# One encoder layer on one core: the first w_ff2 loads wait for a square, and three unused tiles shift addresses

## The chip, the cores and the metric

The kernel runs on one core of a Trainium2 chip. The metric is device time in microseconds (us) from launch to end. A change counts as seen when it goes beyond 0.5%, about what a measurement of this kernel can tell from no change.

## The reference

Input x is 512 tokens by 1024 channels in float32. After a first layer norm one projection of 11,328 columns feeds two branches: 2-D neighbourhood attention (16 heads) and a bidirectional state-space mixer (SSD, 8 groups of 256 channels, each followed by its share of the product with w_ssd_br). Both are merged by sigmoid gates and go through w_o; then comes

```python
h = layer_norm(DN_ALPHA * h + mix, ln1_g[l], ln1_b[l])
h = layer_norm(DN_ALPHA * h + sq_relu_mlp(h, w_ff1[l], w_ff2[l]), ln2_g[l], ln2_b[l])
# sq_relu_mlp(x, w1, w2) = square(relu(x @ w1)) @ w2, w1 1024x4096, w2 4096x1024
```

## The kernel before, in words

**Precision.** Each float32 operand of the large products is split into a high part (rounded to the type fp32r by a copy on ACT) and a low part (the rest, a subtraction on DVE or POOL). `mm3` (lines 351 to 354) then issues three matmuls: high by high, low by high, high by low. In the profile's rows the moving operand is named first behind the arrow and the stationary one second.

**The SSD stage** is planned by the class `Plan`, which orders operations by given costs and issues them in that order. `gated_norm` writes the two halves of a group's result to yTh and yTl; `ssd_branch` multiplies them, as the moving operand (128x512), with w_ssd_br into the banks ps_sbr: 8 groups x 8 output tiles x 2 x 3 = 384 matmuls.

**The MLP** is everything from line 1389. w_ff1 is taken in four quarters of 1024 hidden channels, each in four slabs of 256 columns. `split_weights` loads a slab with one 1 MB DMA on SP's queue into a tile with the tag ws (two buffers), then splits it in two halves: ACT (L341) the high, DVE (L342) the low. `ff1_tile` multiplies 128 hidden channels by all tokens (24 matmuls into one of two banks tagged mm), ACT takes the relu out of the bank (L1554) and the square (L1560) into r2. A bank is free for the next tile but one when its relu is done.

w_ff2 is multiplied by `ff2_strassen` for the first two quarters together (h = 0) and for the third (h = 1), by Strassen's scheme: seven products, in the order 3, 6, 2, 4, 1, 5, 7, in which the squares, or differences of two blocks of squares, are the stationary operand (tiles sqh and sql) and blocks of w_ff2, or sums of two, the moving one. At h = 0 a product has two steps, c = 0 and 1; a step is 24 matmuls. The fourth quarter is done plainly, with gh and gl.

A block of w_ff2 is loaded by `block` (L1448): 1 MB on POOL's queue into a tile w2r. Where a product needs a sum of two blocks, `plus` (L1454) adds the second with two DMAs of 512 KB that accumulate in place; POOL issues them when the first block has landed, so they hold up what follows on POOL's queue. The tiles w2r come from two buffers of their own (tag wr) and, each third one, from the ws buffers that the w_ff1 slabs use too. The first three blocks are those of product 3, step 0 (wr), product 3, step 1 (ws) and product 6, step 0 (wr).

The order within each engine outside the SSD stage is chosen by the framework, which simulates the program and puts what is ready first; each engine then runs its list strictly in order. So a load may be placed well ahead of where the program text has it, and an instruction that waits holds up all that stand behind it on its engine.

**Addresses.** [...] In the kernel before, yTh and yTl begin 64 bytes past a multiple of 128, the four buffers that hold sqh and sql 96 past one, mgh and mgl (the stationary operands of the product with w_o) 96 past one. hTh, hTl, h1Th, h1Tl, aTh, aTl, hBh, hBl, gh, gl and all tiles wh and wl but one pair (one slab of w_o) begin at multiples of 128. The rows of all these tiles are whole multiples of 128 bytes.

Of the kernel before, what the change touches and what calls it, by code (L numbers as in the profile page):

```python
# [11 lines left out]
F32 = mybir.dt.float32  # L12
# [7 lines left out]
P = 128  # L20
# [292 lines left out]
def encoder_layer(ctx, tc, x, w_in, w_attn_br, w_ssd_br, w_o, w_ff1, w_ff2, pcols, rows64,  # L313
                  d_skip, ln_rows, rpb_pad, consts, lmask, out, dbg=None):
    nc = tc.nc
# [11 lines left out]
    def split_weights(parts, nk, ncol, name, hi, lo, eng=nc.vector, pool=None, after=None):  # L327


        st = (pool or wp).tile([P, nk, ncol], F32, tag="ws", name=f"ws_{name}")  # L330
        c = 0
        for src, r0, c0, n in parts:
            nc.sync.dma_start(
                st[:, :, c : c + n],
                src[r0 : r0 + nk * P, c0 : c0 + n].rearrange("(k p) c -> p k c", p=P),
            )
            c += n
        hk = nk // 2
        for i, k in enumerate((slice(0, hk), slice(hk, nk))):
            with tc.issue_after(after[i]) if after else ExitStack():  # L340
                nc.scalar.activation(hi[:, k], st[:, k], AF.Copy)  # L341
            (eng[i] if isinstance(eng, tuple) else eng).tensor_tensor(out=lo[:, k], in0=st[:, k], in1=hi[:, k].bitcast(F32),  # L342
                              op=ALU.subtract)
        return hi, lo
# [6 lines left out]
    def mm3(o, lh, ll, rh, rl, start, stop):  # L351
        nc.tensor.matmul(o, lh, rh, start=start, stop=False)  # L352
        nc.tensor.matmul(o, ll, rh, start=False, stop=False)  # L353
        nc.tensor.matmul(o, lh, rl, start=False, stop=stop)  # L354
# [45 lines left out]
    gcp = gc.__enter__()  # L400
# [3 lines left out]
    gep = ge.__enter__()  # L404
# [2 lines left out]
    ident = cst[:, CC_ID : CC_ID + P]  # L407
    tri_f = cst[:, CC_TF : CC_TF + P]
    tri_b = cst[:, CC_TB : CC_TB + P]
    ones = gcp.tile([P, P], F32, name="ones")  # L410
    nc.vector.memset(ones, 1.0)
    eps = cp.tile([P, 1], F32, name="eps")
# [742 lines left out]
    for pr in range(NH // 2):  # L1155
# [25 lines left out]
        for hh in range(2):  # L1181
            h = 2 * pr + hh
# [91 lines left out]
    for k in range(KD):  # L1274
        ins = nc.scalar.activation(aTh[:, k], aT[:, k], AF.Copy)
# [18 lines left out]
    rx0 = tc.tile_pool(name="rx0", bufs=1, side="right", reuse_waits="tile")  # L1294
    rx0p = rx0.__enter__()
    rows0 = rx0p.tile([P, 2, D], F32, name="rows0")

    def first_norm(t, xt, eng):

        nc.sync.dma_start(xt, x[t * P : (t + 1) * P, :])  # L1300
        mean, rstd = ln0[t]
        eng.tensor_scalar(out=xt, in0=xt, scalar1=mean, scalar2=rstd, op0=ALU.subtract,
                                op1=ALU.mult)
        eng.tensor_tensor(out=xt, in0=xt, in1=rows0[:, 0, :], op=ALU.mult)
        eng.tensor_tensor(out=xt, in0=xt, in1=rows0[:, 1, :], op=ALU.add)
        return xt
# [48 lines left out]
    def ff1_half(w1, j, ps, half):  # L1355

        c = slice(half * 256, (half + 1) * 256)
        for k in range(KD):
            mm3(ps[:, c], w1[0][:, k, j * P : (j + 1) * P], w1[1][:, k, j * P : (j + 1) * P],
                h1Th[:, k, c], h1Tl[:, k, c], k == 0, k == KD - 1)  # L1360
# [10 lines left out]
    for t2 in range(2):  # L1371
# [25 lines left out]
        for t in toks:  # L1397
# [7 lines left out]

    ffp = ctx.enter_context(tc.tile_pool(name="ffp", bufs=1, reuse_waits="tile"))
    NQ = D_FF // D
    pairs = [[gep.tile([P, 4, 256], F32R, tag="gt", bufs=4, name=f"sq{n}_{i}") for n in "hl"]
             for i in range(2)]
    turn = {"parts": 2, "raw": 0}  # L1410

    def parts(name, shape):

        turn["parts"] += 1
        if turn["parts"] % 3 == 0:
            return third(w3p, name, shape)
        return [wp.tile(shape, F32R, tag=n, name=f"{n}_{name}") for n in ("wh", "wl")]

    def raw(name):
        turn["raw"] += 1  # L1420
        pool, tag = ((ffp, "wr"), (ffp, "wr"), (wp, "ws"))[turn["raw"] % 3]
        return pool.tile([P, 4, 512], F32, tag=tag, bufs=2, name=f"w2r_{name}")
# [11 lines left out]
    def ff2_strassen(h, q0, r2):  # L1434
# [1 line left out]


        np_ = len(r2)
        begun, made = set(), [0]

        def rows(i, n, c, k=slice(0, 4)):
            r0 = q0 * D + (i * np_ + c) * 512
            return w_ff2[r0 : r0 + 512, n * 512 : (n + 1) * 512].rearrange(
                "(k p) c -> p k c", p=P)[:, k]

        def block(name, i, n, c):
            t = raw(f"{h}_{name}_{c}")
            nc.gpsimd.dma_start(t, rows(i, n, c))  # L1448
            return [t[:, k] for k in halves]

        def plus(x, i, n, c):
# [57 lines left out]
        def total(name, x, y):  # L1509
            return lambda c: right(name, c, plus(block(name, *x, c), *y, c))  # L1510
# [5 lines left out]
                           (1, 1))  # L1516
        yield from product(2, lambda c: left("2", c, (1, 0), (1, 1)),
                           lambda c: right("2", c, block("2", 0, 0, c)), (1, 0), (1, 1, sub))
        yield from product(4, lambda c: left("4", c, (1, 1)), total("4", (1, 0), (0, 0)),
                           (1, 0), (0, 0))  # L1520
        b11 = []

        def right1(c):
            if not c:
                b11.extend(block("5", 1, 1, i) for i in range(np_))
            t = raw(f"{h}_1_{c}")
            x = [t[:, k] for k in halves]
            for i in range(2):
                nc.scalar.activation(x[i], b11[c][i], AF.Copy, scale=-1.0)
            return right("1", c, plus(x, 0, 0, c))  # L1530
# [7 lines left out]
    def ff1_tile(fq, f, last):  # L1538

        s, j = f // 2, f % 2  # L1540
        if fq == 0 and s < 2:
            w1, ps = early[f]
            ff1_half(w1, j, ps, 1)
        else:
            if j == 0:
                slab[0] = split_weights([(w_ff1, 0, fq * D + s * 256, 256)], KD, 256, f"f1_{fq}_{s}",
                                        *parts(f"f1_{fq}_{s}", [P, KD, 256]))
            w1 = slab[0]
            ps = psx.tile([P, S], F32, tag="mm", bufs=BANKS["mm"], name=f"ps_f1_{fq}_{f}")
            for k in range(KD):  # L1550
                mm3(ps, w1[0][:, k, j * P : (j + 1) * P], w1[1][:, k, j * P : (j + 1) * P],
                    h1Th[:, k, :], h1Tl[:, k, :], k == 0, k == KD - 1)
        rl = ffp.tile([P, S], F32, tag="rl", bufs=2, name=f"rl{fq}_{f}")
        nc.scalar.activation(rl, ps, AF.Relu)  # L1554
        if last:
            nc.vector.tensor_tensor(out=rl, in0=rl, in1=ps, op=ALU.mult)
            nc.scalar.activation(gh[:, f, :], rl, AF.Copy)
            return nc.vector.tensor_tensor(out=gl[:, f, :], in0=rl, in1=gh[:, f, :].bitcast(F32),
                                           op=ALU.subtract)
        return nc.scalar.activation(r2[fq][:, f, :], rl, AF.Square)  # L1560
# [7 lines left out]
    for fq in range(2):  # L1568
        for f in range(KD):
            ins = ff1_tile(fq, f, False)  # L1570
            if fq == 0 and f == 4:

                for t in range(NT):
                    for i, o in ((0, ALU.mult), (1, ALU.add)):
                        aff = nc.gpsimd.tensor_tensor(out=acc[t], in0=acc[t], in1=row1[i], op=o)
                        if t == 0 and i == 0:
                            tc.add_manual_dep(aff.ins, ins.ins.name, mybir.DependencyInfo(
                                mybir.DependencyClass.Sync, mybir.DependencyReason.DATA),
                                reason="behind the first channels")

    r2.append(squares("r2_2"))
    run = ff2_strassen(0, 0, r2[:2])
    for f in range(0, KD, 2):
        for _ in range(3):
# [5 lines left out]

    gh, gl = squares("gh", F32R), squares("gl", F32R)
    run = ff2_strassen(1, 2, r2[2:])
    for f in range(0, KD, 2):
        ff1_tile(3, f, True)
# [3 lines left out]

    r0 = (NQ - 1) * D
    rest = ffp.tile([P, 2, 4, 512], F32R, tag="r2", bufs=3, name="w2_4")  # L1600
# [86 lines left out]
```

## Time and profile before

| | |
|---|---|
| median of 3 runs | 1215.16 us (1214.47 to 1220.26) |
| the profiled execution's own time | 1215.97 us |
| its span, first to last instruction | 1214.2 us |
| mean granted TensorE clock | 0.994 |
| PE / DVE / ACT / POOL busy | 97% / 64% / 50% / 45% |
| w2r DMAs | 18 of 1 MB, 30 of 512 KB, 34.6 MB on POOL's queue |

Times in the views are microseconds from the start of the span. PE's matmuls overlap each other, so a matmul's listed time is longer than the distance between two starts; where the pace matters the document takes the distance between starts. A row of a timeline has start, length, engine, line, operation, what is written and read, and in brackets the idle time before it with what ended it. A row of windows has busy time and number of instructions of each engine in a stretch, the granted clock, the busy share of the 16 DMA engines and the rate at which they moved data.

### The profile page before, as it was taken

The numbers are of one execution on the slowest core, as the hardware profiler recorded it, in microseconds if no ns is written. First come the engines' busy times: TensorE is split into PE (matmuls) and PEld (weight loads), VectorE is DVE, ScalarE is ACT, GpSimd is POOL, SyncE is SP. The second block draws the span as 40 slices with busy tenths as digits, with TensorE's granted clock in tenths as the row PEclk, the third lists the DMA queues.
The fourth block names the chain that finished last, engine by engine and source line by source line (L and its number), as shares of the span: only waits on it lengthen the run. The fifth ranks groups of instructions, "written<-read, shape, count | busy, mean of one in ns | idle before, by whom it ended". The sixth has DMA issues, their size and how long they took to land.

```text
span 1214.2 us, 16823 instructions
## 1 busy us (share of the span) xinstructions
PE 1174.4 (97%) x6306; PEld 1003.2 (83%) x6306; DVE 778.4 (64%) x1427; ACT 609.4 (50%) x1012; POOL 542.3 (45%) x588
## 2 busy tenths in 40 slices
PE   5999999999999999999999989999979999999996
PEld 5988798989888888788888878889968888878885
DVE  7748475665666665534888975356662467498856
ACT  4576573836355563324677873442254454365510
POOL 1158967777788767303666730014251131221000
PEclk9999999999999999999999999999999999999998
DMA  7144243333333342234432333353185586888511
GB/s 230 53 143 139 89 137 104 114 119 117 105 103 116 115 135 70 70 104 100 101 73 63 83 104 105 104 198 96 56 208 153 159 190 184 186 210 214 152 61 52
DMA packets 131169, 149.21 MB, mean 123 GB/s; under 512 B 22928, under 2 KB 105488, under 8 KB 131088
## 3 DMA queue, kind: packets, MB, share of 16 engines
q1 hardware_dynamic: 118032, 113.54, 30.5%
q0 software_dynamic: 13056, 34.61, 12.0%
q8 instruction: 49, 0.80, 0.3%
q14 instruction: 32, 0.26, 0.1%
HBM read 145.90 MB, written 2.23 MB: 122 GB/s over the span
## 4 chain that ended last, share of the span: by engine, by line
PE 80%; DVE 8%; DMA 4%; ACT 4%; issue 3%; POOL 0%; SPq 0%; DVEq 0%; POOLq 0%; ACTq 0%
PE ps_f L352 8%; PE ps_f L354 8%; PE ps_f L353 8%; PE ps_x L352 5%; PE ps_x L354 5%; PE ps_x L353 5%; PE ps_z L352 3%; PE ps_z L353 3%; PE ps_z L354 3%; PE yd L931 2%; PE ps_sbr L352 2%; PE ps_sbr L354 2%; PE ps_sbr L353 2%; DMA w2r<-in_w_ff 2%; PE ps_g L352 2%
## 5 line engine op out<-in xcount | busy, mean ns | idle before, releaser
L740 DVE SCALAR_TENSOR_TENSOR cv<-ps_x,pc,cv 128x511 f32<-128x511 f32 (+1 forms) x128 | 95.8, 749 | 26.0 <-ACT cv L732 22.2
L352 PE MATMUL ps_f<-h1Th,wh_f 128*128 128x512 f32 (+1 forms) x288 | 105.2, 369 | 5.9 <-ACT rl L1554 5.9
L353 PE MATMUL ps_f<-h1Th,wl_f 128*128 128x512 f32 (+1 forms) x288 | 105.4, 368 | 0.0
L354 PE MATMUL ps_f<-h1Tl,wh_f 128*128 128x512 f32 (+1 forms) x288 | 103.8, 369 | 1.1 <-DVE h1Tl L428 1.1
L1460 DVE TENSOR_TENSOR wl_f<-w2r,wh_f 128x1024 fp32r<-128x1024 f32 x42 | 49.7, 1222 | 63.0 <-ACT wh_f L1459 63.0
L352 PE MATMUL ps_z<-wh_z,hTh 128*128 128x256 f32 x256 | 76.0, 297 | 0.8 <-DVE cv L740 0.8
L354 PE MATMUL ps_z<-wl_z,hTh 128*128 128x256 f32 x256 | 72.4, 283 | 0.0
L353 PE MATMUL ps_z<-wh_z,hTl 128*128 128x256 f32 x256 | 72.3, 283 | 0.0
L352 PEld LDWEIGHTS ps_f<-h1Th,wh_f 128*128 128x128 f32 x288 | 54.7, 190 | 15.4 <-ACT rl L1554 6.4
L353 PE MATMUL ps_f<-wh_f,sql 128*128 128x512 f32 x168 | 66.3, 396 | 0.2 <-DVE sql L1460 0.2
L352 PE MATMUL ps_f<-wh_f,sqh 128*128 128x512 f32 x168 | 66.0, 396 | 0.4 <-ACT sqh L1459 0.4
L354 PE MATMUL ps_f<-wl_f,sqh 128*128 128x512 f32 x168 | 66.1, 395 | 0.0
L1448 POOL DMA_DIRECT2D w2r<-in_w_ff x18 | 15.2, 844 | 113.6 <-DVE wl_f L1460 74.0
L342 DVE TENSOR_TENSOR wl_f<-ws_f,wh_f 128x1024 fp32r<-128x1024 f32 x36 | 46.1, 1319 | 29.4 <-ACT wh_f L341 29.4
L1454 POOL DMA_DIRECT2D w2r<-in_w_ff x30 | 36.5, 1455 | 62.4 <-DMA w2r<-in_w_ff 38.8
L1047 DVE TENSOR_TENSOR ysacc<-ps_sbr,ysacc 128x512 f32<-128x512 f32 x56 | 38.4, 689 | 40.1 <-PE ps_sbr L354 39.7
L354 PEld LDWEIGHTS ps_f<-h1Tl,wh_f 128*128 128x128 f32 x288 | 53.7, 190 | 10.1 <-DVE h1Tl L428 1.3
L353 PEld LDWEIGHTS ps_f<-h1Th,wl_f 128*128 128x128 f32 x288 | 54.7, 190 | 8.9
L1319 POOL TENSOR_TENSOR gt<-gt,ysacc 128x512 f32<-128x512 f32 x8 | 12.8, 1602 | 105.1 <-ACT gt L1059 96.9
L341 ACT ACTIVATE wh_f<-ws_f 128x1024 fp32r<-128x1024 f32 x36 | 36.1, 1052 | 45.2 <-PE ps_o L353 22.1
L352 PE MATMUL ps_x<-hTh,wh_bc 128*128 128x512 f32 (+1 forms) x144 | 57.0, 396 | 1.6 <-ACT wh_bc L470 1.6
L1459 ACT ACTIVATE wh_f<-w2r 128x1024 fp32r<-128x1024 f32 x42 | 42.4, 1051 | 31.7 <-DMA w2r<-in_w_ff 19.2
(327 smaller groups left out, 3915.7 us busy)
## 6 DMA issues: line engine op xcount, KB each, us to landing
ws_f<-in_w_ff SPq DMA_DIRECT2D x20, 1024.0 KB
w2r<-in_w_ff POOLq DMA_DIRECT2D x18, 1024.0 KB, 5.6
bc<-acs_d SPq DMA_DIRECT2D x32, 512.0 KB
w2r<-in_w_ff POOLq DMA_DIRECT2D x30, 512.0 KB, 8.4
ws_bc<-in_w_in SPq DMA_DIRECT2D x16, 512.0 KB
ws_x<-in_w_in SPq DMA_DIRECT2D x8, 1024.0 KB
ws_z<-in_w_in SPq DMA_DIRECT2D x8, 1024.0 KB
ws_g<-in_w_in SPq DMA_DIRECT2D x8, 1024.0 KB
```

Source lines behind the costliest of these rows:

```text
L341: nc.scalar.activation(hi[:, k], st[:, k], AF.Copy)
L342: (eng[i] if isinstance(eng, tuple) else eng).tensor_tensor(out=lo[:, k], in0=st[:, k], in1=hi[:, k].bitcast(F32), op=ALU.subtract)
L352: nc.tensor.matmul(o, lh, rh, start=start, stop=False)
L353: nc.tensor.matmul(o, ll, rh, start=False, stop=False)
L354: nc.tensor.matmul(o, lh, rl, start=False, stop=stop)
L740: op("DVE", 0.75, lambda j=j, o=o, n=n: nc.vector.scalar_tensor_tensor(out=acc()[:, o], in0=ps()[:, n], scalar=tap(j), in1=acc()[:, o], op ...
L931: nc.tensor.matmul(yd()[:, c % 2, h * HD : (h + 1) * HD], bc()[:, 1, h, :], xtok()[:, c, h * HD : (h + 1) * HD], start=True, stop=True)
L1047: op("DVE", 0.69, lambda d=d, ps=ps: nc.vector.tensor_tensor(out=ysacc[:, d, :], in0=ps(), in1=ysacc[:, d, :], op=ALU.add), r=[(ps.name, 0 ...
L1448: nc.gpsimd.dma_start(t, rows(i, n, c))
L1454: nc.gpsimd.dma_start(t, rows(i, n, c, k), accum_op=ALU.add)
L1459: nc.scalar.activation(hi[:, k], x, AF.Copy)
L1460: nc.vector.tensor_tensor(out=lo[:, k], in0=x, in1=hi[:, k].bitcast(F32), op=ALU.subtract)
```

## The change

Two edits in one diff. `gc_pad` (64 bytes a partition, ahead of `ones` in the left pool gc), `rx_pad` (32 bytes, behind rows0 in the right pool rx0) and `ge_pad` (96 bytes, in the right pool ge that holds the buffers tagged gt) are never written or read. By the sizes, gc_pad moves all tiles of the SSD stage's pool by 64 bytes, so that yTh and yTl begin at multiples of 128. ge_pad lowers the gt buffers, and with them sqh and sql, by 96 bytes, to multiples of 128; ge_pad and rx_pad together lower mgh and mgl by 128, so these keep their offset.

In `block`, the first three loads of h = 0 get a dependency on `begin`, the square of the second quarter's first tile (ff1_tile(1, 0), on ACT). POOL then waits for that square before it issues any of the three, and issues what stands behind them later too. No instruction is added or taken away beside the waits, and no other load is named.

```diff
+    gcp.tile([P, 16], F32, name="gc_pad")
     ones = gcp.tile([P, P], F32, name="ones")
...
     rows0 = rx0p.tile([P, 2, D], F32, name="rows0")
+    rx0p.tile([P, 8], F32, name="rx_pad")
...
     NQ = D_FF // D
+    gep.tile([P, 24], F32, name="ge_pad")
     pairs = [[gep.tile([P, 4, 256], F32R, tag="gt", bufs=4, name=f"sq{n}_{i}") for n in "hl"]
              for i in range(2)]
...
-        begun, made = set(), [0]
+        begun, made, fetched = set(), [0], [0]
...
         def block(name, i, n, c):
             t = raw(f"{h}_{name}_{c}")
-            nc.gpsimd.dma_start(t, rows(i, n, c))
+            load = nc.gpsimd.dma_start(t, rows(i, n, c))
+            if fetched[0] < 3 and h == 0:
+                tc.add_manual_dep(load.ins, begin.ins.name, mybir.DependencyInfo(
+                    mybir.DependencyClass.Sync, mybir.DependencyReason.DATA),
+                    reason="behind the first quarter's squares")
+            fetched[0] += 1
             return [t[:, k] for k in halves]
...
     for fq in range(2):
         for f in range(KD):
             ins = ff1_tile(fq, f, False)
+            if fq == 1 and f == 0:
+                begin = ins
```

## The prediction

> **What bounds the kernel now.** I read the page's shares first, then what PE waits for, then a table of stretches around the longest wait.
>
> ```profile
> PE 1174.4 (97%) x6306; PEld 1003.2 (83%) x6306; DVE 778.4 (64%) x1427; ACT 609.4 (50%) x1012; POOL 542.3 (45%) x588
> ...
> PE tp_h L561 <- DVE xn L532: 9.8, 1, 9.8
> PE ps_f L352 <- ACT rl L1554: 5.9, 1, 5.9
> ```
>
> PE sets the end: beside its start (9.8 us, untouched here) it waits long only once, 5.9 us for a relu in the first MLP product. So a saving counts only if it shortens that wait or PE's own pace.
>
> ```profile
> 890.00:900.00 10.00, 10.00 (x46) 8.29 (x45) 9.89 (x7) 3.40 (x7) 8.06 (x5) 1.00 1.02 185
> 900.00:910.00 10.00, 4.05 (x18) 3.09 (x17) 2.37 (x3) 3.43 (x5) 0.00 (x0) 0.83 0.86 235
> 910.00:920.00 10.00, 10.00 (x38) 8.08 (x38) 3.56 (x4) 4.97 (x8) 1.02 (x2) 0.82 0.65 210
> 920.00:930.00 10.00, 10.00 (x46) 8.28 (x45) 2.36 (x2) 4.24 (x6) 2.21 (x2) 1.00 0.85 158
> 930.00:940.00 10.00, 10.00 (x46) 8.29 (x45) 2.36 (x2) 4.03 (x6) 0.78 (x1) 1.00 0.22 60
> 940.00:950.00 10.00, 10.00 (x46) 8.29 (x45) 2.36 (x2) 3.39 (x6) 3.19 (x3) 1.00 0.73 177
> 950.00:960.00 10.00, 10.00 (x46) 8.13 (x45) 2.96 (x3) 4.60 (x7) 0.47 (x1) 1.00 0.41 131
> ```
>
> The wait lies at 904 to 910, and the granted clock falls to 0.82 in the 10 us behind it: 1.8 us more. ACT's and POOL's timelines and SP's row tell why.
>
> ```profile
> 892.81 0.60 ACT L1554 ACTIVATE rl<-ps_f 128x512 f32<-128x512 f32 x1 [0.65 <-PE ps_f L354]
> ...
> 906.54 2.00 ACT L341 ACTIVATE wh_f<-ws_f 128x1024 fp32r<-128x1024 f32 x2 [12.47 <-DMA ws_f<-in_w_ff]
> ...
> 908.97 0.58 ACT L1554 ACTIVATE rl<-ps_f 128x512 f32<-128x512 f32 x1
> ...
> 917.83 0.63 ACT L1560 ACTIVATE r<-rl 128x512 f32<-128x512 f32 x1
> ...
> 933.52 0.60 ACT L1554 ACTIVATE rl<-ps_f 128x512 f32<-128x512 f32 x1 [4.18 <-PE ps_f L354]
> 934.01 2.00 ACT L1459 ACTIVATE wh_f<-w2r 128x1024 fp32r<-128x1024 f32 x2
> ...
> 938.96 0.60 ACT L1554 ACTIVATE rl<-ps_f 128x512 f32<-128x512 f32 x1 [2.42 <-PE ps_f L354]
> ```
>
> ```profile
> 881.37 1.81 POOL L1448 DMA_DIRECT2D w2r<-in_w_ff  x2
> ...
> 887.87 5.03 POOL L1454 DMA_DIRECT2D w2r<-in_w_ff  x4
> 892.25 5.89 POOL L1575 TENSOR_TENSOR acc<-acc,row 128x1024 f32<-128x1024 f32 x2
> 914.33 0.81 POOL L1448 DMA_DIRECT2D w2r<-in_w_ff  x1 [16.20 <-DVE wl_f L342]
> ...
> 890.24 2.64 SPq L333 DMA_DIRECT2D ws_f<-in_w_ff  x2
> ...
> DMA to landing us min/median/max: 6.1/10.5/15.1
> ```
>
> ```profile
> 890.24 16.28 DMA ws_f<-in_w_ff
> ...
> 909.60 0.80 PE ps_f L352
> ```
>
> From 881.4 POOL issues blocks and sums of product 3 step 0 and product 6 step 0: 2 x 1 MB and 4 x 0.5 MB. The last row is the landing of the four sums issued from 887.9 to 890.7: up to 15.1 us, so to about 905.8. In that crowd SP asks at 890.24 for the second and third slab of the second quarter, and by the chain of waits (the two rows above) the second takes 16.28 us. ACT has the second slab's split ahead of two relus and stands 12.47 us for it; PE finds both mm banks full until 909.6; it ended the first quarter 5.9 before, at 903.7. 6 MB in the 25 us from 881.4 to 906.5 make 4.2 us for 1 MB with all queues full.
>
> **The pace.** Starts on PE, then the two groups with their counts:
>
> ```profile
> 955.09 0.39 PE L352 MATMUL ps_f<-wh_f,sqh 128*128 128x512 f32 x1
> ...
> 971.88 0.39 PE L352 MATMUL ps_f<-h1Th,wh_f 128*128 128x512 f32 x1
> ...
> 982.77 0.39 PE L352 MATMUL ps_f<-wh_f,sqh 128*128 128x512 f32 x1
> ...
> 478.67 0.39 PE L353 MATMUL ps_sbr<-yTh,wl_sbr 128*128 128x512 f32 x1
> ...
> 486.83 0.40 PE L352 MATMUL ps_g<-hTh,wh_g 128*128 128x512 f32 x1
> ...
> 764.43 0.39 PE L352 MATMUL ps_g<-hTh,wh_g 128*128 128x512 f32 x1
> ...
> 807.96 0.28 PE L352 MATMUL ps_o<-wh_o,mgh 128*128 128x256 f32 x1
> ...
> L353 PE MATMUL ps_f<-wh_f,sql 128*128 128x512 f32 x168 | 66.3, 396 | 0.2 <-DVE sql L1460 0.2
> ...
> L353 PE MATMUL ps_sbr<-yTh,wl_sbr 128*128 128x512 f32 x128 | 50.5, 395 | 0.0
> ```
>
> Three steps of Strassen, 72 matmuls, take 16.79 us: 233.2 ns each. The two w_ff1 tiles behind them, 48, take 10.89: 226.9. 35 matmuls of ps_sbr take 8.16: 233.1; 192 of ps_g 43.53: 226.7. The two slow groups are the two whose operands lie off multiples of 128 (squares 96, yTh and yTl 64), and Strassen and w_ff1 alternate in one stretch, so it isn't the stage.
>
> **The change part by part.**
>
> *The wait.* POOL issues none of the three blocks before the square that stands at 917.83 now. Without the stall that square ends near 910.3: PE ends the first quarter at 903.7, one tile is 5.44 us (933.52 to 938.96), relu and square 1.2. Behind it on POOL stand only the sums and later blocks; the additions of acc (L1575) wait for an earlier square (892.25) and belong ahead of it; were they behind, DVE's sums into acc after the first product would be the first to need them. The third block (product 3 step 1) goes into a ws buffer and is issued at 914.33 now, when DVE has split the slab before it (the idle time's row); the release at 910.3 comes no later. SP's slabs of the third quarter share those buffers and keep their place behind it. Then the second slab has the DMA engines shared with SP's own loads alone: 2 MB at 4.2 us land by 899, even if SP issues no earlier than 890.24, and PE's first quarter lasts to 903.7. Removed: 5.9 us idle, 1.8 us of clock behind 910 and, at the same clock, 0.1 to 0.2 from 909.6 to 910: **7.9 us**.
>
> What is late next: these blocks. ACT's first split of w2r moves from 934.01 to about 926. If blocks and sums run as at 881.4 (two blocks, then the first block's sums, the second of them the median landing, 10.5 us after an issue near 888.7), step 0 of product 3 is whole some 17 us after the release, near 928. If all three blocks go ahead of the first sum and a slab's load shares, 5 MB at 4.2 are 21 us: 931. At the slowest rate of the rows above while sums run (158 GB/s) 4 MB alone take 26 us: 936 or 937. ACT can stand still from 926 to about 933 before PE feels it (2.42 us of idle before the relu at 938.96 and one more bank, 5.44). So the price is 0 by the first two, 4 us by the third, and up to 8 if PE's clock falls again. I take **1.0**: two of three rows end before 933.
>
> *The backlog.* 910 to 960 moved 7.4 MB. The 4 MB come on top, 2 MB of slabs leave: 9.4 MB for the 42 us from 910.3 to 952 (960 less 8). At 4.2 us for 1 MB that takes 39. It fits barely, and later the chain goes over w2r's DMAs with PE right behind:
>
> ```profile
> 1033.01 8.21 DMA w2r<-in_w_ff
> ...
> 1043.86 5.35 DMA w2r<-in_w_ff
> ...
> 1050.57 12.20 DMA w2r<-in_w_ff
> 1062.79 1.07 ACT wh_f L1459
> ```
>
> In those 30 us PE can't end sooner than the DMAs let it, so the faster pace of the matmuls beside them (three steps, 72 x 6.3 ns) is given back: **0.5**. Some backlog may arrive there too, bounds 0 to 4 us (one block); I take **0.8**, near the lower end, because 39 of 42 fits.
>
> *The margins.* If both groups take the pace of the others: squares 3 x 168 x 6.3 ns = 3.2 us, ps_sbr 3 x 128 x 6.4 ns = 2.5, together **5.7**, all on PE, which is never idle in those stretches. Bounds: 0, if the offset isn't the cause, and 5.7; the other tiles that move feed products of other shapes (yd, st, yo), where no row shows both offsets. I take 5.7, since every group of 128x512 fp32r products at a multiple of 128 that I timed starts each 227 ns. [...]
>
> *Sum.* Against the profiled execution's 1215.97 (span 1214.2 and 1.8 around it): -7.9 - 5.7 + 1.0 + 0.5 + 0.8 = -11.3, so 1204.7. The median of the runs lies 0.8 below the profiled one: 1203.9. I say **1204**.
>
> **The rivals.**
>
> 1. *The margins do nothing* (the pace comes from something else that squares and yT share). Against: Strassen and w_ff1 alternate. 1215.2 - 7.9 + 1.0 + 0.8 = 1209.1.
> 2. *The stall moves.* The three blocks bunch behind the square, ACT stands at the first split of w2r past 933, PE waits again with a low clock: 8 us back, as at 904. For: the third rate above. 1204 + 7 = 1211.
> 3. *The change doesn't do what it says*: the slab is late without the blocks too, or the new order puts another load in front of a relu. Only the margins count: 1215.2 - 5.7 + 0.5 = 1210.0. Against: 4 MB of the 6 go.
> 4. *Slower.* The backlog decides: at 158 GB/s the 42 us move 6.6 of 9.4 MB; 2.8 MB are 18 us late at 952. Blocks now land some 10 us before PE needs them (sums issued from 887.9 land by 905.8 for splits from 934 on; the later ones less). So 8 us stay as a wait in product 3, 6 or 2, twice with a lowered clock (2 each) if it comes in two, and again 5 at the stretch 1033 to 1063, where nothing is spare: -13.6 + 8 + 4 + 5 + 0.5 = +4, and with a third slab of a w_ff1 quarter late behind the shared ws buffer (another 4) 1223. It decides only if the rate with sums in flight stays under some 190 GB/s, where 9.4 MB no longer fit in 42 us plus the 8 of slack on ACT; the rows of 900 to 920 show 210 to 235.
>
> **How the numbers follow.** Chances: forecast 0.60, rival 1 0.13, rival 2 0.13, rival 3 0.07, rival 4 0.07. 0.5% (about what a measurement of this kernel can tell from no change) is 6.1 us, so faster means under 1209.1. Forecast (its own range 1201 to 1208) and half of rival 1 and a little of rival 2 and 3 give faster 0.72; rivals 2 and 3 and the rest of 1 give same 0.21; slower 0.07. The range starts at 1200 (all 13.6 us of gains make 1201.6; the rest for what products of other shapes may gain and for the 0.7 us between two of the runs) and ends at 1211.5, past rivals 2 and 3.
>
> **What would show it.** Right: no PE wait of over 1 us for L1554; ACT's wait for ws_f gone; L1448 first issued behind the first square of the second quarter; clock 1.00 from 880 on; starts of ps_sbr and of the squares' products 227 ns apart. Wrong: a wait of ACT's L1459 for DMA w2r of over 7 us right behind the release, followed by PE waiting for L1554 (rival 2); starts at 233 in either group (rival 1); PE waiting for wh_f or wl_f in products 3, 6, 2 (rival 4). A landing of the second slab past 903 would break the first step outright.

## The result and the profile after

The changed kernel takes 1209.35 us in the median of 8 runs (1207.06 to 1212.54), the kernel before 1215.89 beside it on the same chip (8 runs, 1214.35 to 1220.26). The ratio is 0.9938 with an interval from 0.9924 to 0.9953: 6.5 us less. On another chip (the run e7_changed_again below) it is 1206.71 against 1218.11, ratio 0.9905, 0.9891 to 0.9919; the two intervals do not overlap, and why is not known. The profiled execution of the changed kernel took 1207.45 us, 8.5 less than that of the kernel before. In the code, L1554 is now L1562, L1560 L1568, L1459 L1467, L1448 L1451, L1454 L1462 and L1575 L1585.

The waits of PE in the changed kernel (what waited, for whom, us in total, times, longest), the start's first, then the longest of the others, and the one that the experiments come back to:

```profile
PE tp_h L562 <- DVE xn L533: 9.7, 1, 9.7
PE po L1251 <- DVE aT L1265: 2.0, 3, 1.3
...
PE ps_f L352 <- ACT sqh L1467: 0.7, 1, 0.7
```

The wait of 5.9 us for a relu is gone; beside the start nothing is over 2 us. Around its place the windows of the changed kernel (busy time of PE, PEld, DVE, ACT, POOL, then the granted clock, the DMA share and GB/s) are:

```profile
900.00:910.00 10.00, 10.00 (x46) 8.29 (x45) 2.96 (x3) 4.88 (x7) 0.00 (x0) 1.00 0.37 105
910.00:920.00 10.00, 10.00 (x46) 8.29 (x45) 2.36 (x2) 3.61 (x5) 6.46 (x7) 1.00 0.84 288
920.00:930.00 10.00, 10.00 (x46) 8.29 (x45) 1.98 (x2) 3.76 (x5) 3.39 (x3) 1.00 1.08 232
930.00:940.00 10.00, 10.00 (x45) 8.29 (x45) 2.83 (x3) 4.24 (x6) 0.78 (x1) 1.00 1.12 229
```

From 900 to 910 PE is busy 10.00 where it was 4.05, and the clock behind it is 1.00 where it was 0.82. ACT's and POOL's timelines of the changed kernel tell how:

```profile
892.18 0.60 ACT L1562 ACTIVATE rl<-ps_f 128x512 f32<-128x512 f32 x1 [0.66 <-PE ps_f L354]
893.54 2.01 ACT L341 ACTIVATE wh_f<-ws_f 128x1024 fp32r<-128x1024 f32 x2 [0.76 <-DMA ws_f<-in_w_ff]
...
909.13 0.63 ACT L1568 ACTIVATE r<-rl 128x512 f32<-128x512 f32 x1
...
925.31 1.05 ACT L1467 ACTIVATE wh_f<-w2r 128x1024 fp32r<-128x1024 f32 x1
928.15 1.06 ACT L1467 ACTIVATE wh_f<-w2r 128x1024 fp32r<-128x1024 f32 x1 [1.79 <-DMA w2r<-in_w_ff]
```

```profile
910.09 2.55 POOL L1451 DMA_DIRECT2D w2r<-in_w_ff  x3 [13.00 <-ACT r L1568]
916.01 4.96 POOL L1462 DMA_DIRECT2D w2r<-in_w_ff  x4 [3.37 <-DMA w2r<-in_w_ff]
921.94 2.41 POOL L1462 DMA_DIRECT2D w2r<-in_w_ff  x2 [0.97 <-DMA w2r<-in_w_ff]
```

POOL waits for the square at 909.13 and then issues all three blocks. ACT now stands 0.76 us for the second slab, not 12.47, and 1.79 us for product 3, step 0, whole near 928.1. None of that reaches PE. Between the relu at 892.18 (892.81 before) and the release square at 909.13 (917.83 before) the changed kernel gains 8.70 - 0.63 = 8.1 us.

The margins show in the starts on PE (first two rows: 35 matmuls of ps_sbr up to ps_g; last three: three Strassen steps of 72 and then two w_ff1 tiles of 48), and in the groups by line (count, busy us, mean ns of one, idle before), all of the changed kernel:

```profile
475.94 0.39 PE L353 MATMUL ps_sbr<-yTh,wl_sbr 128*128 128x512 f32 x1
...
483.97 0.39 PE L352 MATMUL ps_g<-hTh,wh_g 128*128 128x512 f32 x1
...
946.39 0.40 PE L352 MATMUL ps_f<-wh_f,sqh 128*128 128x512 f32 x1
...
963.13 0.40 PE L352 MATMUL ps_f<-h1Th,wh_f 128*128 128x512 f32 x1
...
974.07 0.40 PE L352 MATMUL ps_f<-wh_f,sqh 128*128 128x512 f32 x1
```

```profile
L353 PE MATMUL ps_f<-wh_f,sql 128*128 128x512 f32 x168 | 66.2, 395 | 0.2 <-DVE sql L1468 0.2
...
L353 PE MATMUL ps_sbr<-yTh,wl_sbr 128*128 128x512 f32 x128 | 50.0, 391 | 0.0
```

ps_sbr: 8.03 us for 35, 229.4 ns each, against 233.1; its mean length falls from 395 to 391 ns. That is not the full step to 227: only the last 18 of the 35, from 479.88 on, start 227 ns apart, the 17 ahead of them 232, and no run shows why. The squares: 16.74 us for 72, 232.5 ns, against 233.2, and 395 against 396. They hardly moved, although their offset did; that is the surprise of this result.

A second thing was not in the prediction. At the end of the attention the windows are these, first of the kernel before and then of the changed kernel (the third number from the end is the clock):

```profile
715.00:720.00 5.00, 2.83 (x21) 2.36 (x21) 2.36 (x8) 2.16 (x5) 1.11 (x1) 1.00 0.00 0
720.00:725.00 5.00, 4.46 (x19) 3.42 (x20) 4.97 (x12) 5.00 (x9) 0.00 (x0) 1.00 0.98 315
```

```profile
715.00:720.00 5.00, 3.62 (x13) 3.04 (x13) 2.54 (x8) 3.17 (x6) 0.00 (x0) 0.50 0.30 109
720.00:725.00 5.00, 5.00 (x20) 4.00 (x19) 5.00 (x8) 3.59 (x6) 0.00 (x0) 0.83 0.76 312
```

In windows of 0.5 us the clock of the changed kernel is 0.50 in each from 715.0 to 721.5 and 1.00 in each from 722.0 on. So a mean clock of 0.50 and 0.83 over 5 us each is 5.0 + 1.7 = 6.7 us at half speed. Experiments e5 and e7 price it.

### The profile page after: what moved, and what is told of

Read it like the earlier page. It is cut to its first block, busy times and chain, and to the rows that moved or that the text cites. A ratio compares the mean times of both kernels' runs of the same rounds, so it can differ in the third digit from the quotient of the medians.

```text
span 1205.7 us, 16822 instructions
## 1 busy us (share of the span) xinstructions
PE 1172.6 (97%) x6306; PEld 1004.4 (83%) x6306; DVE 780.4 (65%) x1427; ACT 608.9 (51%) x1012; POOL 541.9 (45%) x588
## 4 chain that ended last, share of the span: by engine, by line
PE 85%; DVE 5%; ACT 3%; DMA 3%; issue 3%; POOL 1%; SPq 0%; DVEq 0%; POOLq 0%; ACTq 0%
PE ps_f L354 8%; PE ps_f L353 8%; PE ps_f L352 8%; PE ps_x L354 5%; PE ps_x L352 5%; PE ps_x L353 5%; PE ps_z L352 3%; PE ps_z L353 3%; PE ps_z L354 3%; PE yd L932 2%; DMA w2r<-in_w_ff 2%; PE ps_sbr L352 2%; PE ps_sbr L354 2%; PE ps_sbr L353 2%; PE ps_g L352 2%
## 5 line engine op out<-in xcount | busy, mean ns | idle before, releaser
L1462 POOL DMA_DIRECT2D w2r<-in_w_ff x30 | 36.3, 1416 | 70.2 <-DMA w2r<-in_w_ff 46.2
L1467 ACT ACTIVATE wh_f<-w2r 128x1024 fp32r<-128x1024 f32 x42 | 42.5, 1052 | 34.4 <-DMA w2r<-in_w_ff 22.0
L1451 POOL DMA_DIRECT2D w2r<-in_w_ff x18 | 16.1, 896 | 92.3 <-DVE wl_f L1468 55.8
L352 PE MATMUL ps_sbr<-yTh,wh_sbr 128*128 128x512 f32 x128 | 55.6, 434 | 1.2 <-DVE ysacc L1048 0.6
```

The source lines that it names most:

```text
L1451: load = nc.gpsimd.dma_start(t, rows(i, n, c))
L1462: nc.gpsimd.dma_start(t, rows(i, n, c, k), accum_op=ALU.add)
L1467: nc.scalar.activation(hi[:, k], x, AF.Copy)
```

## The experiments

**The wait alone, and the margin of yTh and yTl alone.** Run on one chip with the kernel before (median 1217.27).

```diff
# e1_wait_only: the changed kernel without its margins
-    gcp.tile([P, 16], F32, name="gc_pad")
-    rx0p.tile([P, 8], F32, name="rx_pad")
-    gep.tile([P, 24], F32, name="ge_pad")
# e2_gc_pad_only: the kernel before with one margin
+    gcp.tile([P, 16], F32, name="gc_pad")
```

> The wait of the three loads alone, without the three margins. Theory: the wait removes the stall at 904 to 910 by itself and the margins do nothing to it, so PE's 5.9 us wait for L1554 is gone, the clock stays at 1.00 from 880 to 960, ps_sbr starts stay 233 ns apart and the squares' products 233. Time: 8 us under before, some 1207.5 to 1208. Rival (the margins bring most, the stall is only moved): under 3 us.

> gc_pad alone: yTh and yTl at multiples of 128, squares still 96 past one, no wait. Theory: ps_sbr goes from 233 to 227 ns, 2.5 us by the end of the SSD stage; the stall at 904 stays; squares stay at 233.3. Time 2.5 us under before, 1213. Rival (the gain at ps_sbr is lost again in the attention stage, which waits for DVE and ACT): within 0.5 us of before, and the shift of 2.5 us is there at 509 us and gone at 760.

e1 is 1209.34 in the median of 5 (1205.33 to 1210.26), ratio 0.9935 (0.9922 to 0.9949), 7.9 us less. Its window at the old stall shows the whole step of the wait, with no margin; then its starts of ps_sbr:

```profile
900.00:910.00 10.00, 10.00 (x46) 8.28 (x45) 2.96 (x3) 4.88 (x7) 0.43 (x1) 1.00 0.33 103
```

```profile
477.68 0.40 PE L353 MATMUL ps_sbr<-yTh,wl_sbr 128*128 128x512 f32 x1
...
485.85 0.40 PE L352 MATMUL ps_g<-hTh,wh_g 128*128 128x512 f32 x1
```

e2 is 1214.6 in the median of 8, ratio 0.9980 (0.9966 to 0.9994), 2.7 us less. Its stall is untouched, and ps_sbr has the changed kernel's length:

```profile
PE ps_f L352 <- ACT rl L1555: 5.9, 1, 5.9
```

```profile
L353 PE MATMUL ps_sbr<-yTh,wl_sbr 128*128 128x512 f32 x128 | 50.0, 391 | 0.0
```

So in the traces each part does alone what it does in the changed kernel. The times don't show that the two add up: e1, without any margin, is 1209.34 and the changed kernel 1209.35, on different chips, and the two never ran side by side. e1 also warns of a reading: its row at 477.68 is 0.99 us earlier than before's 478.67 with no margin at all. Of the 2.73 us that the changed kernel has gained there (475.94), some 1.7 (477.68 - 475.94) belong to the margin; by the mean length, 395 to 391 ns for 384 products, it is 1.5. What brings the other 0.99 is not known.

**Why the squares stay slow: banks, or the margin of mgh.** The first theory after the result was that the squares' products lose their time by changing between two banks in the inner loop. The second run leaves out rx_pad, which moves no operand timed here but mgh and mgl.

```diff
# e3_one_bank: the changed kernel, in ff2_strassen
-                for k in range(4):
-                    for j in range(2):
+                for j in range(2):
+                    for k in range(4):
# e4_no_rx_pad: the changed kernel
-    rx0p.tile([P, 8], F32, name="rx_pad")
```

> The changed kernel with the two inner loops of a Strassen step swapped: 12 matmuls into one bank, then 12 into the other, in place of 3 and 3. Same arithmetic, same operands at the same addresses. Theory: the slow pace of the squares' products (232.4 ns with all operands at multiples of 128) comes from the change of bank after each third matmul; then starts are 227 ns apart and 504 matmuls save 2.7 us: 1206.6 where the changed kernel has 1209.35. Rival (it comes from where the squares lie, or from ACT and DVE writing beside them): 232 stays and the time is that of the changed kernel.

> The changed kernel without rx_pad: mgh and mgl, the stationary operands of the product with w_o, begin at multiples of 128 in place of 96 past one. If the offset of a stationary operand sets the pace at all, the 384 products 128x256 of ps_o leave their 117 to 118 ns (to the 120 of the other 128x256 groups, 0.8 to 1.1 us more in all); if it doesn't, they stay.

e3's starts on PE, at the same three places:

```profile
949.73 0.40 PE L352 MATMUL ps_f<-wh_f,sqh 128*128 128x512 f32 x1
...
966.48 0.40 PE L352 MATMUL ps_f<-h1Th,wh_f 128*128 128x512 f32 x1
...
977.41 0.40 PE L352 MATMUL ps_f<-wh_f,sqh 128*128 128x512 f32 x1
```

16.75 us for 72, 232.6 ns: the theory of the banks falls. e3's median is 1205.82 (5 runs, ratio 0.9911, 0.9897 to 0.9926); the changed kernel did not run on that chip, so nothing is claimed from its time. e4 took 1205.01 in its one run, and its products with mgl went from 282 to 283 ns of mean length, a difference too small to read.

**Multiples of 256 bytes.** What is left is where the tiles lie. Their addresses say something that the prediction had not looked at: both operands of every group of 128x512 products timed at 227 ns start at a multiple of 256 bytes, and so do yTh and yTl after gc_pad (192 past one before). The squares start 128 bytes past one after ge_pad (224 before). The expectations below call 256 bytes the unit. Three runs test it from both sides; a fourth repeats the changed kernel on the same chip (kernel before: 1218.11).

```diff
# e5_ge_224: the changed kernel, squares at multiples of 256
-    gep.tile([P, 24], F32, name="ge_pad")
+    gep.tile([P, 56], F32, name="ge_pad")
# e6_ge_224_no_rx: the same, and mgh and mgl at multiples of 256 too
-    rx0p.tile([P, 8], F32, name="rx_pad")
# e8_gc_192: the changed kernel, yTh and yTl 128 past a multiple of 256
-    gcp.tile([P, 16], F32, name="gc_pad")
+    gcp.tile([P, 48], F32, name="gc_pad")
```

> The changed kernel with a margin of 224 bytes ahead of the squares in place of its own, so that sgl and sgh start at multiples of 256 bytes; mgh and mgl, behind them, come to 224 bytes past such a multiple, as in the kernel before. Theory (256 bytes is the unit): the three series of 168 squares go from 232.4 ns from start to start to 227 ns, 504 x 5.4 ns = 2.7 us less than the changed kernel on the same chip. Rival (the place of the squares or the reads of other engines beside them set their pace, not the offset): 232 ns stays, and the time is the changed kernel's within 0.5 us.

> As the run before, with the margin ahead of rx left out, so that mgh and mgl too start at multiples of 256 bytes. Theory (256 bytes is the unit): squares at 227 ns; the 128x256 products that read mgh and mgl, 117 ns before and in the changed kernel and 118 to 119 ns at 128 past a multiple, come to about 113 ns if the unit counts for them as it does for the wide ones, and to about 120 ns if they go as the other 128x256 groups at a multiple do. Rival (place or other readers): squares 232 ns, these products 117 to 118 ns.

> The changed kernel with a margin of 192 bytes ahead of yTh and yTl in place of its own, so that they start 128 bytes past a multiple of 256. Theory (256 bytes is the unit): the 384 products into ps_sbr go back from 227 ns to about 232 ns, 384 x 5 ns = 2 us more than the changed kernel. Rival (multiples of 128 bytes are enough for the moving operand, and the squares are slow for another reason): 227 ns stays.

> The changed kernel once more, on the chip of these runs: 6 to 9 us under the kernel before. Theory (a loss of the clock near 715 us comes in some executions and not in others): single times spread over 2 us or more, and the profile shows either half clock near 715 us and a span near 1205.5 us, or full clock there and a span near 1203 us. Rival (the margins bring that loss every time): half clock near 715 us again, and no single time under 1206 us.

e5's starts on PE:

```profile
943.96 0.39 PE L352 MATMUL ps_f<-wh_f,sqh 128*128 128x512 f32 x1
...
960.28 0.39 PE L352 MATMUL ps_f<-h1Th,wh_f 128*128 128x512 f32 x1
...
971.16 0.39 PE L352 MATMUL ps_f<-wh_f,sqh 128*128 128x512 f32 x1
```

16.32 us for 72, 226.7 ns, and 226.7 for the w_ff1 tiles behind them: the squares have the pace of all others. The groups by line of e6, and then of e8:

```profile
L353 PE MATMUL ps_f<-wh_f,sql 128*128 128x512 f32 x168 | 65.3, 390 | 0.2 <-DVE sql L1467 0.2
...
L353 PE MATMUL ps_o<-wh_o,mgl 128*128 128x256 f32 x128 | 36.1, 283 | 0.0
```

```profile
L353 PE MATMUL ps_sbr<-yTh,wl_sbr 128*128 128x512 f32 x128 | 50.5, 394 | 0.0
```

In e6 the squares are at 390 ns too. In e8 ps_sbr goes back to 394, a multiple of 128 though it is; its 35 matmuls take 233 ns again. So the theory holds for the stationary squares, which 128 bytes made fast, and for the moving yTh and yTl, which 128 bytes made slow again. One thing these runs can't tell: by the tiles' addresses every fast operand, the squares of e5 and yTh and yTl after gc_pad included, lies 256 bytes past a multiple of 512. No run put one of these operands at a multiple of 512, so multiples of 256 in general are not shown to be fast. The theory does not hold for the 128x256 products: at a multiple of 256, mgl stays at 283, as at 128 past one (e4).

e5 is 1204.64 (4 runs, ratio 0.9888, 0.9875 to 0.9902) and e7, the changed kernel, 1206.71: 2.1 us for the 2.7 expected; their two intervals overlap, so the pace is shown by the starts, not by these times. e6 took 1204.85 and e8 1206.13 in one run each; the 2 us that e8 was to cost against e7 can't be seen in its time.

**The half clock near 715.** e7 is the changed kernel, instruction for instruction. Its windows, then the same two matmuls on PE in the changed kernel's first profile, in e7 and in e5 (a product of the attention and the seventh of ps_abr behind it):

```profile
715.00:720.00 5.00, 3.62 (x16) 2.88 (x16) 3.19 (x10) 3.61 (x7) 0.00 (x0) 0.77 0.49 171
720.00:725.00 5.00, 5.00 (x21) 4.14 (x20) 5.00 (x7) 3.14 (x5) 0.00 (x0) 0.89 0.62 250
```

```profile
714.46 0.36 PE L1251 MATMUL po<-pth,vhl 128*128 128x256 f32 x1 [1.33 <-DVE aT L1265]
...
720.83 0.63 PE L353 MATMUL ps_abr<-aTh,wl_abr 128*128 128x512 f32 x1
```

```profile
714.75 0.36 PE L1251 MATMUL po<-pth,vhl 128*128 128x256 f32 x1 [1.33 <-DVE aT L1265]
...
720.38 0.63 PE L353 MATMUL ps_abr<-aTh,wl_abr 128*128 128x512 f32 x1
```

```profile
714.61 0.36 PE L1251 MATMUL po<-pth,vhl 128*128 128x256 f32 x1 [1.33 <-DVE aT L1265]
...
719.20 0.40 PE L353 MATMUL ps_abr<-aTh,wl_abr 128*128 128x512 f32 x1
```

6.37 us, 5.63 and 4.59: half clock costs 1.8 us there in the first execution (6.7 us of it) and 1.0 in e7 (0.77 and 0.89, so 2.3 + 1.1 = 3.4 us of it), beside e5 with a clock of 1.00. The wait ahead, 1.33 us, is the same in all three, so the same waits lose the clock in one execution and not in another. No margin settles it: e4, with two of them, and e5 and e8, with all three, show 1.00 there, and e3, e6, e9, e10 and e11, with two or three, half clock. Whether the margins make it likelier is open: the three traces with neither ge_pad nor rx_pad (before, e1, e2) all show 1.00.

The clock also differs between executions from 15 to 25 us: 0.66 in e11, 1.00 in e10, in the changed kernel's first profile and in that of the kernel before. So single times can differ for reasons that no edit here made. What sets the moment at which the clock falls or comes back, no run shows.

**How late may the blocks come, and what the faster squares meet.** The last three runs hold the blocks two tiles longer, alone and together with e5's margin; e5 is repeated beside the latter (kernel before there: 1215.86).

```diff
# e9_third_tile: the changed kernel; e10_later_and_256: e5; e11_256_again: e5 unchanged
-            if fq == 1 and f == 0:
+            if fq == 1 and f == 2:
                 begin = ins
```

> The changed kernel with the first three blocks of w_ff2 held two tiles longer, for the square of the second quarter's third tile, near 920.0 in place of 909.1. It measures how much room the step 'what is late next' had. Theory (the blocks come with the queues nearly to themselves, 19 us after the release for product 3, step 0, as in the changed kernel): step 0 whole near 939, ACT stands 2 to 3 us at the first split of w2r, PE waits under 0.5 us before 951, and the time is the changed kernel's on a chip like the last one's, 1203 to 1208 us. Rival (the rate with sums in flight is nearer 158 GB/s, 26 us for 4 MB): step 0 near 946, ACT stands 10 us, and PE waits 2 to 6 us before 955 with a lowered clock behind it, 1208 to 1215 us.

> Two edits together: the margin of 224 bytes (squares at multiples of 256) and the release by the square of the second quarter's third tile. With the first alone PE waited 2.3 us near 1053 for blocks of w_ff2 and lost the clock behind it, 3.2 us in all; with the second alone there was no wait there. Theory (the DMAs of w2r set that wait, and the later release moves the loads out of each other's way): no wait over 0.5 us near 1053, squares at 227 ns, 3 us less than with the margin alone, near 1202. Rival (the wait there comes from the faster squares, which ask for the blocks sooner than the DMAs bring them): the wait of 1 to 3 us is there again, and the time is that with the margin alone within 0.7 us.

> The margin of 224 bytes alone once more, on the chip of the run beside it: 11 to 14 us under the kernel before, 1203 to 1206 us, squares at 227 ns, with a wait of 1 to 3 us near 1053 if it belongs to the kernel, and none if it comes in some executions only.

ACT's timeline of e9 (the release square is the row at 920.88):

```profile
920.88 0.63 ACT L1568 ACTIVATE r<-rl 128x512 f32<-128x512 f32 x1
...
939.03 1.06 ACT L1467 ACTIVATE wh_f<-w2r 128x1024 fp32r<-128x1024 f32 x1 [0.40 <-DMA w2r<-in_w_ff]
941.70 1.06 ACT L1467 ACTIVATE wh_f<-w2r 128x1024 fp32r<-128x1024 f32 x1 [1.61 <-DMA w2r<-in_w_ff]
944.14 1.06 ACT L1467 ACTIVATE wh_f<-w2r 128x1024 fp32r<-128x1024 f32 x1 [1.38 <-DMA w2r<-in_w_ff]
945.11 0.58 ACT L1562 ACTIVATE rl<-ps_f 128x512 f32<-128x512 f32 x1
```

Step 0 is whole near 939.0, 17.5 us after the square's end, as the theory had it. ACT stands 0.4 + 1.6 + 1.4 us, the relu at 945.11 comes some 3 us late, and PE waits for nothing there. One run took 1206.51. So the changed kernel's release has at least 11 us of room.

e5's faster squares meet something else. Its chain of waits before 1056, and the window behind it:

```profile
1032.32 5.40 DMA w2r<-in_w_ff
...
1038.34 0.73 POOL w2r L1462
1039.07 12.52 DMA w2r<-in_w_ff
...
1051.62 1.07 ACT wh_f L1467
```

```profile
1055.00:1060.00 5.00, 4.51 (x12) 3.39 (x13) 4.87 (x9) 3.40 (x6) 0.28 (x2) 0.66 0.67 216
```

A block of w_ff2 and the second half of the sum into it take 5.40 and 12.52 us, ACT's split and a stationary tile (sqh) come behind them, and PE, now ahead, waits 2.3 us for it and then runs 3.4 us at half clock (0.66 over 5 us). The same wait is 0.7 in the changed kernel's first execution, 0.5 in e7, 1.0 in e6 and e11, where the squares are fast too, and not there in e9. e10 has 390 ns of mean length in the squares, as e6 has, and two waits of 0.2 us at this place; it is 1204.43 in the median (6 runs, ratio 0.9906, 0.9889 to 0.9923), e11 1206.13 (6 runs, 0.9918, 0.9904 to 0.9932). That is 1.7 us between the theory's 3 and the rival's 0.7, and the single times overlap (1203.22 to 1207.32, 1205.09 to 1207.77). e11 itself came out 9.7 us under the kernel before and not the forecast 11 to 14, where the same kernel as e5 was 13.5 under on its chip; so what the faster squares are worth in the whole time is not pinned down. That the faster squares run into the chain of w2r's DMAs is shown (2.3, 1.0 and 1.0 us in e5, e6 and e11, at most 0.7 with slow squares); that the later release is what eases it is not settled, since e5 and e11 are the same kernel and differ by 1.3 us in this wait alone.

## Why the prediction was right, and where it was not

It gave 1204.0 and a range of 1200 to 1211.5, and 0.72 for a gain over 0.5%. The time is 1209.35 on one chip and 1206.71 on another, both in the range; the gain is 0.62% on the first (interval 0.47 to 0.76, so its lower end is under 0.5%) and 0.95% on the second. The time alone doesn't speak for the forecast: rival 1, without any gain of the margins, gave 1209.1, nearer to the first chip's 1209.35 than 1204. What is right is the wait, by the traces. Against the profiled execution the forecast was 11.3 us less, and 8.5 came. By its own steps:

- **The wait, 7.9 us.** Right: 8.1 in the profile, 7.9 in e1's median, which has nothing else. The release at 909.8 (forecast 910.3), no relu that PE waits for, the clock of 1.00 from 880 to 960 and ACT's wait for the second slab (0.76 left of 12.47) are as forecast. That slab's split starts at 893.54, well before 903.7.
- **What is late next, price 1.0.** Its landings were right (near 928, found 928.1), its price was not needed: 0. The worst row that it used, 158 GB/s with sums in flight, did not come; 920 to 940 ran at 229 to 232. e9 shows why it was cheap: the blocks could come 11 us later still. Rival 2 is out, and so is rival 4.
- **The backlog, 0.8, and the faster pace given back at 1033 to 1063, 0.5.** PE's waits for sqh and sql there are 0.7 + 0.2 us, before 0.4 + 0.2: together 0.3 of 1.3. The mechanism is real, and its size seems to go with the pace: where the squares are as fast as forecast, 2.3 us and the clock are lost at that place in e5 and 1.0 us in e6 and e11.
- **The margins, 5.7 us.** This is the step that failed, in its second half. ps_sbr: forecast 3 x 128 x 6.4 ns = 2.5; measured 1.5 to 1.7, by the mean length and by 475.94 against e1's 477.68. Squares: forecast 3 x 168 x 6.3 ns = 3.2; measured 504 x 0.7 ns = 0.35. The sentence that failed is that every group I timed at 227 ns starts at a multiple of 128. It was true and did not say what it was used for: they all start at multiples of 256 too, and no row of the trace before told the two apart. e5 and e8 did, and they leave open whether multiples of 512 are fast as well. Rival 1 (the margins do nothing) so holds, but for 0.35 us, for the squares and fails for ps_sbr.
- **Not in the sum.** Half clock near 715 took some 1.8 us of the profiled execution. It comes and goes between executions; it belongs in the range, not in the sum.

The sum from the rows: -8.1 - 1.7 - 0.35 + 0.3 + 1.8 = -8.05 for the 8.5 measured; the rest is of the size of what e1 differs from the kernel before at 477 with the same instructions there. Against the profiled execution the forecast missed 2.8 us: the squares (2.9), ps_sbr (0.8) and the clock (1.8) are too little gain or too much loss, and it was luck that prices that were not needed (1.0 for what is late next and 1.0 of the 1.3 for the backlog and the pace) hid 2.0 of it. The first chip's median lies another 1.9 us above the profiled execution, and no trace shows why.

## What to carry to other kernels

When several groups differ in pace and in an address, list the addresses modulo more than one power of two before you price a shift: the property that all fast groups share may be stronger than the one you wrote down; here even 256 bytes may not be the last word. A load that lands long before its use and competes with one that is due costs the wait of the due one (here 12.47 us of ACT's and 5.9 of PE's, against 0.76 and none with the load held back); hold it back by a dependency, and measure the room with a second, later release. A gain in pace counts only up to the next place where a chain of transfers sets the end (in e5 a wait of 2.3 us behind a DMA of 12.52), and that place is worth finding in the profile first.

## What the runs showed of the hardware

- Products of 128x512 in fp32r with the squares as stationary operand start each 226.7 ns when the squares begin at a multiple of 256 bytes (e5; 256 past a multiple of 512, as every fast operand here), 232.5 at 128 past one (the changed kernel) and 233.2 at 224 (before). With yTh and yTl as moving operand it is 229.4 ns over 35 starts at a multiple of 256, 227 over the last 18 of them, and 233 at 128 (e8) or 192 (before) past one. 128x256 products with mgl showed no such step (281 to 283 ns of length at 224, 128 and 0).
- PE's clock fell to half for 6.7 us (the changed kernel's first profile) or 3.4 (e7) behind the same waits of 1.33 and 1.38 us that left it at 1.00 in e5; 6.7 us cost 1.8, 3.4 cost 1.0, and PE stood still for a part of that time.
- In e5 POOL issued four sums of 512 KB from 1038.34 on (4.89 us for the four); the one that PE's wait hung on took 12.52 us to land. The load of 1 MB before them took 5.40.
